# Half-by-half down projections, more plain tiles and in-place right factors in a hybrid decoder trunk

## The chip, the cores and the metric

The kernel runs on one core of a Trainium2 chip. The metric is the device time of one launch in microseconds. The core's engines are TensorE (PE; its weight loads are shown as PEld), VectorE (DVE), ScalarE (ACT), GpSimd (POOL) and SyncE (SP), which here issues all transfers.

## The reference

Two layers over 1024 prompt tokens and 8 sample tokens (1032 columns, model width 1024). Layer 0 mixes with windowed attention beside a recurrence (the even mixer), layer 1 with a gated chunk mixer (the odd mixer). Each mixer is followed by a ConvFFN of width 2816 (22 tiles of 128 rows). Every part is normed before and after:

```python
def conv_ffn(xn, conv_state, w_gate, w_up, conv_w, conv_b, w_down):
    gpre = xn @ w_gate
    ext = concatenate([conv_state, gpre], axis=1)
    conv = conv_b + conv_w[2] * ext[:, 2:2 + t]
    for j in range(2):
        conv = conv + conv_w[j] * ext[:, j:j + t]
    h = gelu(conv, approximate=True) * (xn @ w_up)
    return h @ w_down, ext[:, -2:]

for layer in range(2):
    m = even_mix(rmsnorm(h), ...) if layer % 2 == 0 else chunk_gmlp_mix(rmsnorm(h), ...)
    h = h + rmsnorm(m)
    h = h + rmsnorm(conv_ffn(rmsnorm(h), ...))
```

All data are float32. Besides the two outputs of the trunk, states and caches are returned.

## The kernel before

**Arithmetic.** Activations lie with features on the partitions and tokens along the columns. Every float32 operand is split into a high part, rounded to fp32r, and a low part (`split`, L283 to L286: ACT makes the high part, DVE or POOL subtracts it). A product is three matmuls, high by high, high by low, low by high (`mm3`, L288 to L291).

**Tokens.** The ConvFFN and the odd mixer treat the tokens in two halves: A is chunk 0 (512 columns), B is chunks 1 and 2 (256 and 264 columns). The operand of half A lies in the tiles `xA`, that of B in `xB`.

**ConvFFN.** `FFN_STEPS` lists the steps of each ConvFFN; `ffn` (L539) walks it.
- `up` steps (`gate_up`, *plain tiles*): gate and up projection of one 128-row tile f for one half. All A steps come first, then all B steps. The weights are split once, stored in DRAM (`wk<-w`), and reread for half B (`w<-wk`). The result h, split in two parts, goes to DRAM (`hd`).
- `pair` steps (`pair`, `both`): two tiles f, f+1 together over all tokens by seven block products instead of eight: the weight pair is a 2 by 2 block matrix (tile by half of the 1024 input rows), and so is the activation (half of the input rows by half of the 1032 tokens, blocks of 516 columns). The seven left factors are formed per pair from raw weights `wa` (`wfactor`, in VectorE's `ws` and in place). Three of the right factors are blocks of x themselves; the other four are sums of blocks and are made once per ConvFFN: `combos` makes three of them in `ta`, `yA`, `yB` and stores the fourth in DRAM (`t4d`), and `combo4` reads and splits it into `xB` buffers that the last plain B step has freed. `combos` is called after the first B step.
- `down` steps (`down`): `load_h` reads h back into `ta`, `gb`, `cb`; the products of the listed tiles add up in PSUM and are then added to y (`yA` for half A, `yB` for half B, L718). After the last one of a chunk, `Boundary.chunk` does the norm after the ConvFFN, the residual and, in the first one, the norm ahead of the odd mixer, whose operand it writes.

Before, the first ConvFFN has 6 plain tiles and 8 pairs, the second 4 and 9. Tiles 0 to 17 go down two at a time over all tokens, tiles 18 to 21 together, first for half A, then for half B.

**Buffers.** Tag `s` has four buffers, which `xc` (blocks of x in `combos`), `wa`, and the residual and norm tiles of the boundaries share. `ta`, `yA`, `yB` have four each, `gb`, `cb`, `ub` two each. Split weights rotate through 8 + 10 buffers of 128 by 512; the weights of a `down` tile take four. Weights are requested three loads ahead in plain and down steps, seven in pairs.

**Order.** The framework fixes the order of each engine's queue in advance, by priority in program order and by its own estimate of when things are ready. On the chip each engine runs its queue in that order and waits on semaphores. SP issues every transfer, so a transfer that must wait holds up those behind it.

Of the kernel before, what the change touches and what calls it, by code (L numbers as in the profile page):

```python
# [9 lines left out]
F32 = mybir.dt.float32  # L10
F32R = mybir.dt.float32r
# [5 lines left out]
P = 128  # L17
# [8 lines left out]
NF = 22  # L26
# [97 lines left out]
def trunk(ctx: ExitStack, tc: tile.TileContext, A, O):  # L124
# [375 lines left out]
    def ft(tag, n=TW, dt=F32):  # L500
        return pools[tag].tile([P, n], dt, tag=tag, name=nm(tag), bufs=FBUFS.get(tag, 1))
# [28 lines left out]
    def ffn(l, xs, raw, bnd):  # L530
# [29 lines left out]
        def gate_up(f, half):  # L560

            t0, n = FCH[half[0]][0], sum(FCH[c][1] for c in half)
            row = ft(("gb", "cb", "ub")[f % 3])
# [29 lines left out]
        def combos():  # L593

            xs.fill()
            for k in range(4):
                x = []
                for i, t0 in ((k, 0), (k, 2 * NQ), (4 + k, 0), (4 + k, 2 * NQ)):
                    t = stile("xc")[:, 0:2 * NQ]
                    SP.dma_start(out=t, in_=raw[i * P:(i + 1) * P, t0:t0 + 2 * NQ])  # L600
                    x.append(t)
                if k % 2 == 0:
                    for i, tag in enumerate(("ta", "yA", "yB")):
                        for part in range(2):
                            tt[i, part, k // 2] = ft(tag, TW, F32R)
                t3 = stile("t3", "g")[:, 0:2 * NQ]
                DVE.tensor_tensor(out=t3, in0=x[3], in1=x[1], op=ALU.subtract)
                DVE.tensor_tensor(out=x[1], in0=x[1], in1=x[0], op=ALU.subtract)
                DVE.tensor_tensor(out=x[3], in0=x[3], in1=x[1], op=ALU.subtract)
                DVE.tensor_tensor(out=x[2], in0=x[2], in1=x[3], op=ALU.subtract)  # L610
                SP.dma_start(out=t4d[k], in_=x[2])
                for i, src in enumerate((x[1], x[3], t3)):
                    split(src, *(tt[i, part, k // 2][:, k % 2 * 2 * NQ:(k % 2 + 1) * 2 * NQ] for part in range(2)),
                          POOL if i == 0 else DVE)
# [72 lines left out]
        def load_h(f):  # L687

            for s, half in enumerate(HALVES):
                t0, n = FCH[half[0]][0], sum(FCH[c][1] for c in half)  # L690
                for part in range(2):
                    t = ft("ta" if f % 4 == 0 else ("gb", "cb")[s], TW, F32R)
                    SP.dma_start(out=t[:, 0:2 * n].bitcast(F32).rearrange("p (i t) -> p i t", i=2),
                                 in_=hd[part][f:f + 2, :, t0:t0 + n].rearrange("i p t -> p i t"))
                    for c in half:
                        for i in range(2):
                            o = i * n + FCH[c][0] - t0
                            hs[f + i, c, part] = t[:, o:o + FCH[c][1]]

        def down(fs, cs, first, last):  # L700
            for f in range(fs[0], min(fs[-1] + 4, NF), 2):
                if (f, cs[0], 0) not in hs:
                    load_h(f)
# [19 lines left out]
        for kind, fs, cs in FFN_STEPS[l]:  # L723
            if kind == "up":
                gate_up(fs, cs)
                if cs == HALVES[1] and not ready:
                    combos()
                    ready = 1
            elif kind == "pair":
                if ready == 1:  # L730
                    combo4()
                    ready = 2
                pair(fs)
            else:
                down(fs, cs, 0 in fs, NF - 1 in fs)
# [38 lines left out]
def _ffn_steps(a, b):  # L774
# [7 lines left out]
    L = tuple(range(NF - b, NF))  # L782
    return s + [("down", L, A), ("down", L, B)]


FFN_STEPS = [_ffn_steps(*a) for a in ((6, 4), (4, 4))]
# [1025 lines left out]
```

## Time and profile before

| | |
|---|---|
| median of 3 runs | 2622.96 us (2621.48 to 2625.72) |
| the profiled execution's own time | 2619.32 us |
| its span, first to last instruction | 2617.5 us |
| mean granted TensorE clock | 0.961 |
| transfers | 509.33 MB, mean 195 GB/s |

How to read the views. Times are us from the span's start unless marked ns. A row of the timeline gives start, duration, engine, line, operation, out<-in with the program's tile names, partitions x elements, and in brackets the engine's idle time before it and what ended that. A row of the windows gives, for one stretch, the busy time of each engine with its number of instructions, then the granted share of TensorE's clock, the busy share of the 16 DMA engines and GB/s. Matmuls are pipelined: a matmul's duration overlaps the next one's, so the pace is read from starts. In the order of time the span has the even mixer (to about 840, overlapped by the first A steps from 719 on), the first ConvFFN (to 1508), the odd mixer (to 1910, overlapped by the second ConvFFN's A steps) and the second ConvFFN.

### The profile page before, as it was taken

The page shows a single profiled execution, that of the slowest core. Times are in us where ns is not written, and L with a number is a line of the kernel's source. Part 1 is how long each engine was busy: PE and PEld are TensorE (multiplying, and loading weights), DVE is VectorE, ACT ScalarE, POOL GpSimd, SP SyncE. Part 2 cuts the span into 40 slices and gives each one's busy share as a digit, 9 for nine tenths or more (in the row PEclk, how much of TensorE's full clock was granted, in tenths as well). Part 3 has the DMA queues.
Part 4 walks back from the last instruction along what each step waited for, and adds up shares of the span by engine and source line. Part 5 has one row for each costly group of instructions (what it writes and reads, how often), then busy time and mean ns, then how long its engine had stood idle before and what let it go on. Part 6 is the DMA issues. An engine that isn't in the chain of part 4 may idle for free. (4 is left out here: it accounts for less than half of the span.)

```text
span 2617.5 us, 50052 instructions
## 1 busy us (share of the span) xinstructions
PE 2446.7 (93%) x18604; PEld 2266.3 (87%) x18604; DVE 1643.1 (63%) x3571; ACT 986.9 (38%) x1941; POOL 873.5 (33%) x947
## 2 busy tenths in 40 slices
PE   6889998999887989999999979999978999999996
PEld 5788888888775989999999868998878999999996
DVE  5776859666764566676455566526566667654556
ACT  4453545444342344444311144434434444441111
POOL 1511123110333255555322253202425555542221
PEclk9899999999798999999999989999989999999998
DMA  9776767765599832323644688665963232354455
GB/s 317 266 241 209 218 193 233 223 213 161 192 345 330 271 107 100 120 92 125 232 133 152 225 283 278 206 190 193 331 214 120 89 120 90 110 190 154 146 186 186
DMA packets 310676, 509.33 MB, mean 195 GB/s; under 512 B 50784, under 2 KB 94368, under 8 KB 310432
## 3 DMA queue, kind: packets, MB, share of 16 engines
q1 hardware_dynamic: 310432, 506.14, 58.3%
q8 instruction: 146, 2.39, 0.4%
q14 instruction: 98, 0.80, 0.1%
HBM read 337.15 MB, written 166.22 MB: 192 GB/s over the span
## 5 line engine op out<-in xcount | busy, mean ns | idle before, releaser
L286 POOL TENSOR_TENSOR w<-raw,w 128x512 fp32r<-128x512 f32 x212 | 288.5, 1371 | 623.4 <-ACT w L285 573.0
L289 PE MATMUL l<-xA,w 128*128 128x258 f32 (+1 forms) x896 | 297.3, 333 | 19.8 <-ACT w L285 15.8
L285 ACT ACTIVATE w<-raw 128x512 fp32r<-128x512 f32 x232 | 143.1, 629 | 453.5 <-PE l L290 317.9
L291 PE MATMUL l<-xA,w 128*128 128x258 f32 (+1 forms) x896 | 295.9, 331 | 1.2 <-POOL w L286 1.0
L290 PE MATMUL l<-xA,w 128*128 128x258 f32 (+1 forms) x896 | 296.2, 331 | 0.6 <-DVE xA L286 0.6
L289 PE MATMUL le<-xs,w 128*128 128x256 f32 (+1 forms) x896 | 270.2, 302 | 24.9 <-ACT w L285 18.3
L289 PE MATMUL l<-xB,w 128*128 128x256 f32 (+2 forms) x976 | 277.4, 287 | 15.1 <-ACT xB L285 14.4
L290 PE MATMUL l<-xB,w 128*128 128x256 f32 (+2 forms) x976 | 279.4, 287 | 0.8 <-DVE xB L286 0.7
L291 PE MATMUL l<-xB,w 128*128 128x256 f32 (+2 forms) x976 | 278.9, 286 | 0.0
L291 PE MATMUL le<-xs,w 128*128 128x256 f32 (+1 forms) x896 | 268.6, 301 | 9.1 <-POOL w L286 6.0
L290 PE MATMUL le<-xs,w 128*128 128x256 f32 (+1 forms) x896 | 265.0, 296 | 0.6 <-DVE xs L286 0.6
L286 POOL TENSOR_TENSOR w<-wa,w 128x512 fp32r<-128x512 f32 x136 | 214.8, 1586 | 65.3 <-ACT w L285 65.3
L289 PEld LDWEIGHTS le<-xs,w 128*128 128x128 f32 x896 | 178.2, 199 | 38.0 <-ACT w L285 21.5
L289 PEld LDWEIGHTS l<-xA,w 128*128 128x128 f32 x896 | 171.6, 192 | 37.5 <-ACT w L285 18.3
L289 PEld LDWEIGHTS l<-xB,w 128*128 128x128 f32 x976 | 186.1, 192 | 16.4 <-ACT xB L285 15.4
L286 POOL TENSOR_TENSOR w<-ws,w 128x512 fp32r<-128x512 f32 x102 | 145.9, 1430 | 162.4 <-ACT w L285 144.4
L291 PEld LDWEIGHTS le<-xs,w 128*128 128x128 f32 x896 | 177.7, 199 | 17.4 <-POOL w L286 7.8
L290 PEld LDWEIGHTS l<-xB,w 128*128 128x128 f32 x976 | 187.0, 192 | 1.7 <-DVE xB L286 1.5
L291 PEld LDWEIGHTS l<-xB,w 128*128 128x128 f32 x976 | 187.2, 192 | 0.0
L291 PEld LDWEIGHTS l<-xA,w 128*128 128x128 f32 x896 | 171.0, 191 | 17.3 <-POOL w L286 1.8
L290 PEld LDWEIGHTS l<-xA,w 128*128 128x128 f32 x896 | 171.1, 191 | 16.0 <-DVE xA L286 1.3
L289 PE MATMUL l<-ta,w 128*128 128x512 f32 (+2 forms) x576 | 184.6, 320 | 0.1
(496 smaller groups left out, 6812.2 us busy)
## 6 DMA issues: line engine op xcount, KB each, us to landing
w<-wk SPq DMA_DIRECT2D x544, 256.0 KB, 4.0
wk<-w SPq DMA_DIRECT2D x320, 256.0 KB, 3.8
raw<-in_down_dram SPq DMA_DIRECT2D x88, 256.0 KB, 4.3
hd<-cb SPq DMA_DIRECT2D x34, 516.0 KB, 4.0
hd<-ub SPq DMA_DIRECT2D x34, 516.0 KB, 4.0
wa<-in_gate_dram SPq DMA_DIRECT2D x68, 256.0 KB, 2.8
wa<-in_up_dram SPq DMA_DIRECT2D x68, 256.0 KB, 2.6
ta<-hd SPq DMA_DIRECT2D x24, 520.0 KB, 5.4
```

Of the source, the lines that this page charges most:

```text
L285: ACT.activation(out=hi, in_=src, func=AF.Copy)
L286: (eng or DVE).tensor_tensor(out=lo, in0=src, in1=hi.bitcast(F32), op=ALU.subtract)
L289: PE.matmul(out, wh, xh, start=start, stop=False, **kw)
L290: PE.matmul(out, wh, xl, start=False, stop=False, **kw)
L291: return PE.matmul(out, wl, xh, start=False, stop=stop, **kw)
```

## The change

Three edits in the ConvFFN:

1. `FFN_STEPS`: plain tiles from 6 to 8 in the first ConvFFN and from 4 to 6 in the second (one pair fewer in each). The last eight tiles, not the last four, go down half by half: tiles 14 to 17 for A, 18 to 21 for A, 14 to 17 for B, 18 to 21 for B. `load_h` loads the halves that the present step and the next one need, through `ta`, `gb`, `ta`, `cb` in turn.
2. Plain tiles use the row buffers `gb` and `cb` in turn, no longer `ub`.
3. `combos` reads three of the four block rows two row blocks at a time into buffers of `ta`, `yA` and `yB` themselves (for both row pairs ahead), uses `ub` for two sums, and writes the split factors over buffers of the same tags. Only the fourth block passes through `xc`.

```diff
@@ gate_up
-            row = ft(("gb", "cb", "ub")[f % 3])
+            row = ft(("gb", "cb")[f % 2])
@@ combos
-            for k in range(4):
-                x = []
-                for i, t0 in ((k, 0), (k, 2 * NQ), (4 + k, 0), (4 + k, 2 * NQ)):
-                    t = stile("xc")[:, 0:2 * NQ]
-                    SP.dma_start(out=t, in_=raw[i * P:(i + 1) * P, t0:t0 + 2 * NQ])
-                    x.append(t)
-                if k % 2 == 0:
-                    for i, tag in enumerate(("ta", "yA", "yB")):
-                        for part in range(2):
-                            tt[i, part, k // 2] = ft(tag, TW, F32R)
-                t3 = stile("t3", "g")[:, 0:2 * NQ]
-                DVE.tensor_tensor(out=t3, in0=x[3], in1=x[1], op=ALU.subtract)
-                DVE.tensor_tensor(out=x[1], in0=x[1], in1=x[0], op=ALU.subtract)
-                DVE.tensor_tensor(out=x[3], in0=x[3], in1=x[1], op=ALU.subtract)
-                DVE.tensor_tensor(out=x[2], in0=x[2], in1=x[3], op=ALU.subtract)
-                SP.dma_start(out=t4d[k], in_=x[2])
-                for i, src in enumerate((x[1], x[3], t3)):
-                    split(src, *(tt[i, part, k // 2][:, k % 2 * 2 * NQ:(k % 2 + 1) * 2 * NQ] for part in range(2)),
-                          POOL if i == 0 else DVE)
+            tags, W = ("ta", "yA", "yB"), 2 * NQ
+            def load(t, k, right, cnt):
+                SP.dma_start(out=cols(t, cnt, W), in_=rows(raw, k, cnt, right * W, W))
+                return t[:, 0:cnt * W]
+            x = {k: [load(ft(tag), r, right, 2) for tag, r, right in zip(tags, (k, k, 4 + k), (0, 1, 1))] for k in (0, 2)}
+            for k in (0, 2):
+                for i, tag in enumerate(tags):
+                    for part in range(2):
+                        tt[i, part, k // 2] = ft(tag, TW, F32R)
+                x11, x12, x22 = x[k]
+                t1, t2 = (ft("ub")[:, 0:2 * W] for _ in range(2))
+                DVE.tensor_tensor(out=t1, in0=x12, in1=x11, op=ALU.subtract)
+                DVE.tensor_tensor(out=t2, in0=x22, in1=t1, op=ALU.subtract)
+                for i in range(2):
+                    one = slice(i * W, i * W + W)
+                    t3 = stile("t3", "g")[:, 0:W]
+                    DVE.tensor_tensor(out=t3, in0=x22[:, one], in1=x12[:, one], op=ALU.subtract)
+                    x21 = load(stile("xc"), 4 + k + i, 0, 1)
+                    DVE.tensor_tensor(out=x21, in0=x21, in1=t2[:, one], op=ALU.subtract)
+                    SP.dma_start(out=t4d[k + i], in_=x21)
+                    split(t3, *(tt[2, part, k // 2][:, one] for part in range(2)), POOL)
+                for i, t in enumerate((t1, t2)):
+                    split(t, *(tt[i, part, k // 2][:, 0:2 * W] for part in range(2)))
@@ load_h, down, the walk over the steps
-        def load_h(f):
-            for s, half in enumerate(HALVES):
-                t0, n = FCH[half[0]][0], sum(FCH[c][1] for c in half)
-                for part in range(2):
-                    t = ft("ta" if f % 4 == 0 else ("gb", "cb")[s], TW, F32R)
...
+        halfs = [0]
+        def load_h(fs, cs):
+            for half in HALVES:
+                t0, n = FCH[half[0]][0], sum(FCH[c][1] for c in half)
+                for f in fs[::2] if half[0] in cs and (fs[0], half[0], 0) not in hs else ():
+                    for part in range(2):
+                        t = ft(("ta", "gb", "ta", "cb")[halfs[0] % 4], TW, F32R)
...
+                    halfs[0] += 1
-            for f in range(fs[0], min(fs[-1] + 4, NF), 2):
-                if (f, cs[0], 0) not in hs:
-                    load_h(f)
+                for _, f, c in FFN_STEPS[l][k:k + 2]:
+                    load_h(f, c)
@@ _ffn_steps
-    L = tuple(range(NF - b, NF))
-    return s + [("down", L, A), ("down", L, B)]
-FFN_STEPS = [_ffn_steps(*a) for a in ((6, 4), (4, 4))]
+    return s + [("down", tuple(range(f, f + 4)), half) for half in (A, B) for f in range(NF - b, NF, 4)]
+FFN_STEPS = [_ffn_steps(*a) for a in ((8, 8), (6, 8))]
```

## Rows read from the trace of the kernel before

**Rows 1.** The page: busy time, share and instructions of each engine.
```profile
PE 2446.7 (93%) x18604; PEld 2266.3 (87%) x18604; DVE 1643.1 (63%) x3571; ACT 986.9 (38%) x1941; POOL 873.5 (33%) x947
```
**Rows 2.** Windows, plain B steps and pairs: PE, PEld, DVE, ACT, POOL, clock, DMA share, GB/s.
```profile
860.00:910.00 50.00, 50.00 (x419) 50.00 (x418) 29.68 (x50) 17.60 (x38) 8.37 (x9) 1.00 0.89 286
...
1000.00:1200.00 200.00, 200.00 (x1667) 199.95 (x1667) 139.15 (x197) 84.69 (x137) 108.54 (x89) 1.00 0.31 106
```
**Rows 3.** Timeline of TensorE, ten consecutive matmuls of an A step, first and last.
```profile
1867.82 0.40 PE L291 MATMUL l<-xA,w 128*128 128x512 f32 x1
...
1869.90 0.39 PE L291 MATMUL l<-xA,w 128*128 128x512 f32 x1
```
**Rows 4.** Windows at the ConvFFNs' beginnings and ends, columns as in rows 2.
```profile
840.00:850.00 10.00, 0.00 (x0) 0.00 (x0) 0.74 (x2) 0.63 (x1) 0.18 (x1) 0.69 1.06 382
850.00:860.00 10.00, 8.95 (x49) 8.65 (x50) 5.60 (x8) 5.72 (x10) 3.33 (x8) 0.62 0.82 249
...
910.00:950.00 40.00, 33.32 (x257) 32.49 (x257) 23.92 (x36) 17.30 (x37) 20.87 (x18) 0.96 0.41 134
...
1500.00:1530.00 30.00, 15.40 (x86) 13.22 (x85) 24.63 (x40) 12.58 (x22) 18.27 (x13) 0.72 0.82 279
1890.00:1920.00 30.00, 18.12 (x111) 16.70 (x111) 19.41 (x53) 7.83 (x14) 6.15 (x5) 0.72 0.73 243
1950.00:2040.00 90.00, 75.15 (x568) 73.72 (x567) 53.91 (x77) 35.06 (x61) 44.07 (x39) 0.91 0.37 120
```
**Rows 5.** Timeline of TensorE, the longest waits in these windows.
```profile
850.91 0.58 PE L289 MATMUL l<-xB,w 128*128 128x256 f32 x1 [12.33 <-ACT xB L285]
...
942.69 0.44 PE L289 MATMUL l<-yB,w 128*128 128x258 f32 x1 [4.08 <-DVE gb L654]
...
1513.89 1.84 PE L331 MATMUL pp<-cst,sq 128*128 128x1 f32 x8 [5.60 <-DVE sq L325]
1522.68 1.08 PE L352 MATMUL pp<-cst,pp 128*128 128x128 f32 x4 [6.96 <-DVE pp L310]
1525.34 2.07 PE L289 MATMUL l<-xA,w 128*128 128x512 f32 x4 [1.57 <-ACT xA L285]
...
1904.33 1.11 PE L331 MATMUL pp<-cst,sq 128*128 128x1 f32 x6 [7.79 <-DVE sq L329]
...
1962.23 0.58 PE L289 MATMUL l<-xA,w 128*128 128x258 f32 x1 [5.88 <-ACT w L285]
```
**Rows 6.** Timeline of SP's queue, end of `combos` in the second ConvFFN.
```profile
1953.64 0.32 SPq L600 DMA_DIRECT2D xc<-xne  x1
1958.45 2.95 SPq L214 DMA_DIRECT2D wa<-in_gate_dram  x2
```
**Rows 7.** Timeline of VectorE, three places.
```profile
1482.96 0.69 DVE L718 TENSOR_TENSOR yA<-yA,l 128x512 f32<-128x512 f32 x1 [0.64 <-PE l L291]
...
1969.96 0.69 DVE L220 TENSOR_TENSOR ws<-wa,wa 128x512 f32<-128x512 f32 x1 [5.73 <-DMA wa<-in_gate_dram]
...
2598.37 0.43 DVE L329 TENSOR_TENSOR sq<-sq 128x264 f32<-128x264 f32 x1
```
**Rows 8.** The page's DMA issues: number, KB each, us from issue to landing.
```profile
w<-wk SPq DMA_DIRECT2D x544, 256.0 KB, 4.0
wk<-w SPq DMA_DIRECT2D x320, 256.0 KB, 3.8
...
ta<-hd SPq DMA_DIRECT2D x24, 520.0 KB, 5.4
```
**Rows 9.** Windows: last four tiles' down projections, half A into half B.
```profile
1480.00:1500.00 20.00, 19.87 (x157) 19.27 (x155) 12.04 (x30) 3.51 (x6) 5.49 (x5) 1.00 0.46 151
```
**Rows 10.** Timeline of TensorE, the end: sums of the last two norms.
```profile
2593.68 0.50 PE L331 MATMUL pp<-cst,sq 128*128 128x1 f32 x4
...
2604.07 1.11 PE L331 MATMUL pp<-cst,sq 128*128 128x1 f32 x6 [3.41 <-DVE yB L472]
```
**Rows 11.** Windows: ten us of the first A steps, beside the even mixer's end.
```profile
730.00:740.00 10.00, 9.72 (x60) 8.54 (x60) 8.01 (x23) 5.06 (x12) 2.54 (x2) 1.00 1.06 393
```

More of the change, by code (lines that the diff above doesn't have):

```diff
@@ L685, in pair @@
                 keep(f + i, u, c, u, 0)
-        def load_h(f):
-            for s, half in enumerate(HALVES):
+        halfs = [0]
+        def load_h(fs, cs):
+            for half in HALVES:
                 t0, n = FCH[half[0]][0], sum(FCH[c][1] for c in half)
-                for part in range(2):
-                    t = ft("ta" if f % 4 == 0 else ("gb", "cb")[s], TW, F32R)
[L693 to L698, printed above, removed]
+                for f in fs[::2] if half[0] in cs and (fs[0], half[0], 0) not in hs else ():
+                    for part in range(2):
+                        t = ft(("ta", "gb", "ta", "cb")[halfs[0] % 4], TW, F32R)
+                        SP.dma_start(out=t[:, 0:2 * n].bitcast(F32).rearrange("p (i t) -> p i t", i=2),
+                                     in_=hd[part][f:f + 2, :, t0:t0 + n].rearrange("i p t -> p i t"))
+                        for c in half:
+                            for i in range(2):
+                                o = i * n + FCH[c][0] - t0
+                                hs[f + i, c, part] = t[:, o:o + FCH[c][1]]
+                    halfs[0] += 1
         def down(fs, cs, first, last):
-            for f in range(fs[0], min(fs[-1] + 4, NF), 2):
-                if (f, cs[0], 0) not in hs:
-                    load_h(f)
             ws = [wget(f"down{l}", f) for f in fs]
@@ L722, in ffn @@
         ready = 0
-        for kind, fs, cs in FFN_STEPS[l]:
+        for k, (kind, fs, cs) in enumerate(FFN_STEPS[l]):
             if kind == "up":
```

## The prediction

> **What bounds the kernel now.** The page comes first: TensorE is busy 93% of the span, no other engine over 63% [rows 1]. A mean over unlike stages says little, so next come windows over the stages. Inside the ConvFFNs TensorE has no idle time at all: 419 matmuls in 50 us of plain B steps, 1667 in 200 us of pairs, so 0.120 us for one of 256 to 264 columns [rows 2]; one of 512 columns starts every 0.231 us (nine starts in 2.08 us) [rows 3]. There the count of matmuls is the time, and only doing fewer or narrower ones helps. All that is lost around these stages is lost at five joints [rows 4], and the timeline of TensorE says what each waits for [rows 5]. The loss of a joint is its window minus matmuls times pace.
>
> - **J1**, first ConvFFN, A steps to B steps (838 to 860): 12.33 us without a matmul, waiting for the operand `xB` of half B; then 49 matmuls (5.9 us at full pace) in the 9.1 us left of the window, at a granted clock of 0.62: 3.2 us. 15.5 us.
> - **J2**, its first pair: 40 - 257 x 0.120 = 9.2 us, the largest wait for VectorE's adds of `gb`.
> - **J3**, first ConvFFN to odd mixer: 74 wide matmuls of its 86, 63 x 0.120 + 11 x 0.231, and 0.4 for the small ones, 10.5 us in 30: 19.5 us, mostly the norm of half A (5.60 and 6.96 us before its sums and its spread), partly clock (0.72).
> - **J4**, second ConvFFN, A to B: 96 wide ones of its 111, 84 x 0.120 + 12 x 0.231, and 0.6 for the small, 13.5 us in 30: 16.5 us; 7.79 us of it before the norm's sums of the last chunk.
> - **J5**, its first pairs: 90 - 568 x 0.120 = 21.8 us; the largest wait (5.88) is for a weight's split.
>
> Together 82.5 us. The end is a sixth place: the norm of half B after the last matmul.
>
> **Two more plain tiles per ConvFFN.** One pair is replaced by two plain tiles. A pair issues 2 x 7 x 4 x 3 x 2 = 336 matmuls: 40.3 us. A plain tile issues 48 of 512 columns (11.1 us, an A step) and 96 of 256 or 264 (11.5 us, a B step), so two take 45.2 us. Price: 4.8 us per ConvFFN, **+9.6 us**, certain wherever TensorE is the bound. The Trainium skill (TensorE: Matmul & The Clock Gate, section Back-to-back issue gap) speaks for a lower price: it gives a sustained 131 ns for N=512. By that an A step would be 6.3 us and the swap would give back 4.7 us per ConvFFN instead of costing 4.8; the trace has 231 ns in these fp32r streams, so the measurement decides and the sum keeps +9.6.
>
> What it buys is independent work. J1 and J4 open because the A steps run out (6 and 4 of them) before half B's operand is there. Two more give 22.2 us of matmuls that need half A alone, against joints of 15.5 and 16.5 us, slow clock included. Bounds: nothing regained (15.5 and 16.5 stay) to everything. The added A tile is not free for the queues: 1.05 MB of raw weights, 2.1 MB of split weights kept in DRAM and 0.5 MB of result, 3.7 MB in 11.1 us or 330 GB/s, while J1's windows already move 382 and 249 GB/s. I leave 4 us at J1 and 3 at J4: **-11.5 and -13.5**.
>
> The two more B steps come after `combos` was called, so the right factors and the first pair's weights get 23 us more before they are needed. This counts for J2 and J5, below.
>
> **Row buffers.** Plain tiles now use `gb` and `cb` alone: four rows instead of six. A row lives from its first eviction, through one step, to the landing of its store, some 20 us; four last four steps, over 44 us. Cost 0, hidden by the steps between; if stores took 20 us longer it would be a wait per step.
>
> **Right factors in place.** Before, the 16 `xc` loads go through the four buffers of tag `s`, which the raw weights `wa` of the pairs need too. SP shows it: the last `xc` is issued at 1953.64, the first `wa` at 1958.45 [rows 6], and VectorE waits until 1969.96 for a gate weight [rows 7]. After, twelve of the sixteen blocks go straight into `ta`, `yA`, `yB`, and only four pass through `s`. The arithmetic stays (the same subtractions and splits, many twice as wide, so fewer instructions); the loads are six of double size and four single ones. So `wa` can be loaded during the B steps. SP runs past six larger loads early in the B steps; the weights behind them are three loads ahead, so a delay of a few us is covered. In-place use adds one wait: the low parts of the second row pair's third factor must wait until the block beneath was read, about 3 us on POOL, behind which only further splits queue; with five further B steps, 58 us, or more until the first pair it is covered. What stays late is the fourth factor, which needs the last plain step's buffers, and its four splits on VectorE. I leave 3 us at J2 and 4 at J5: **-6.2 and -17.8**. Bounds: 0 to -31 together.
>
> **Last eight down projections by halves.** The `hd` loads now run one step ahead instead of two; a step lasts 22 us and a load lands in 5.4 [rows 8], so 0. The same number of matmuls comes in four-tile steps A1, A2, B1, B2 instead of two-tile steps and one A, one B step. Half A is now complete 46 us (384 x 0.120) before half B, formerly 23 us. Its norm took from its last add at 1482.96 [rows 7] to the first matmul of the next stage at 1525.34, 42.4 us, so it nearly fits beneath B1 and B2 and J3 almost closes. Against it: four more tiles' weights are split, stored and read again, 4.2 MB each way, beside the norm's 4 MB of loads and stores; J3's window moves 279 GB/s as it is. Bounds 0 and -19.5; I take **-14.5**. Partial sums are added 24 times fewer per ConvFFN; VectorE was not the bound there, so 0.
>
> A step of four tiles holds 16 of the 18 weight buffers, so the next one's weights come late. The one such joint that a ConvFFN has before shows no loss in the first: 19.87 of 20 us busy [rows 9]. But its second half was a reread, while A1 to A2 also needs ACT's and POOL's splits, and B1 frees its buffers only in its second chunk. Four new joints, 0 to 12.7 us each (4.2 MB at 330 GB/s); nearer the row at 0: **+5** in all.
>
> In the last ConvFFN the same step moves half A's norm away from the end. There the last chunk's squares are summed at 2598.8 [rows 7], but TensorE's sums start at 2604.07, because the bank is still read for the chunk before [rows 10], and that one was late behind half A's work. **-5**, bounds 0 and -8.
>
> **Sum.** 9.6 + 5 - 11.5 - 6.2 - 14.5 - 13.5 - 17.8 - 5 = -53.9. The profiled execution took 2619.3 us (span 2617.5 and 1.8 around it): 2565.4. The median of the runs is 3.6 higher: 2569. All bounds at their best (-82.5 - 8 + 9.6) give 2542.
>
> **The rivals.**
> - *R1, DMA is the limit at the joints.* The change adds 64 kept stores and 64 rereads to 320 and 544 [rows 8], 33.6 MB at 262 KB each. Then the added transfers push back what J1, J3 and J4 wait for, and these three stay: -53.9 + 11.5 + 14.5 + 13.5 = -14.4, 2609. For it: J1's wait lies in a window at full DMA share. Against it: the A steps before J4 keep their pace [rows 3]. The Trainium skill (DMA: Bandwidth & Descriptors, section Bandwidth) puts HBM's limit per core near 358 GB/s; by that 33.6 MB would be 94 us of transfers, had they no cover. The trace has 393 GB/s over 10 us [rows 11], above that figure.
> - *R2, TensorE's fixed order.* Its queue is written in advance; if the norm's sums stand ahead of the new A steps, TensorE still waits at J1 and J4 with work behind: -53.9 + 25 = -28.9, 2594. For it: J4's wait is exactly at such sums, `pp<-cst,sq`. Against it: the queue had no other work to put there.
> - *R3, the first pairs are late for other reasons* (VectorE's in-order queue): J2 and J5 stay, -53.9 + 24 = -29.9, 2593. For it: J2's largest wait is VectorE's. Against it: J5's largest is a weight.
> - *R4, slower.* No weight of a four-tile step arrives before the step ahead of it ends: 12.7 us at six joints, 76 us instead of 5: -53.9 + 71 = +17, 2640. It decides from 9.8 us a joint on (58.9 / 6). Against it: the existing joint at no loss.
>
> **How the numbers follow.** Forecast 0.57 (its own range 2545 to 2588), R1 0.12, R2 0.12, R3 0.10, R4 0.06, no net change 0.03. 0.2% (5 us) is about what a measurement of this kernel tells from no change. Faster is all but R4, the no-change case and a part of R1: 0.89; same 0.03; slower 0.08. The range runs from the best bounds to past R2 and R3, leaving out R4 and most of R1: 2542 to 2604.
>
> **What would show it.** Right: no TensorE wait over 3 us between A and B steps in either ConvFFN; `wa` issued during the B steps; TensorE busy between the last down projection and the odd mixer; 18508 matmuls with more busy time in the ConvFFNs; 384 kept stores, 608 rereads; the end within 20 us of the last wide matmul. Wrong: waits on `w<-wk` or on splits at A1 to A2 or B1 to B2 (R4); waits for `xB` with DMA at full share (R1); waits at `pp<-cst,sq` with A steps behind (R2).

## The result, and the profile after

The changed kernel takes 2595.15 us (median of 4 runs, 2588.62 to 2601.36); the kernel before, run beside it, 2624.34 us (2621.48 to 2625.99). The ratio is 0.989, 95% interval 0.9863 to 0.9916: some 29 us faster, where 54 were forecast. The time lies in the range given (2542 to 2604), near its slow end, and outside the range that the forecast gave for itself (2545 to 2588). The profiled execution took 2596.03 us, its span 2594.2 us against 2617.5.

The page of the changed kernel, TensorE's line and three lines of the DMA issues (number, KB each, us from issue to landing):

```profile
PE 2450.8 (94%) x18508; PEld 2263.8 (87%) x18508; DVE 1600.0 (62%) x3471; ACT 982.8 (38%) x1937; POOL 863.2 (33%) x943
...
w<-wk SPq DMA_DIRECT2D x608, 256.0 KB, 4.1
wk<-w SPq DMA_DIRECT2D x384, 256.0 KB, 3.7
...
ta<-hd SPq DMA_DIRECT2D x36, 512.0 KB, 4.6
```

96 matmuls fewer than in [rows 1], 64 kept stores and 64 rereads more than in [rows 8]: the change does what it says. Windows of the changed kernel, columns as in [rows 2]:

```profile
860.00:910.00 50.00, 34.01 (x237) 32.37 (x238) 31.73 (x40) 18.91 (x34) 14.38 (x17) 0.86 1.01 360
870.00:880.00 10.00, 4.81 (x24) 4.56 (x24) 8.87 (x7) 3.42 (x5) 4.05 (x2) 0.60 1.06 393
960.00:1010.00 50.00, 50.00 (x417) 49.93 (x416) 32.70 (x50) 23.39 (x44) 26.40 (x24) 1.00 0.27 87
1440.00:1460.00 20.00, 16.19 (x63) 12.51 (x62) 4.67 (x9) 4.41 (x8) 4.80 (x4) 0.91 1.03 389
1460.00:1510.00 50.00, 43.77 (x310) 41.52 (x309) 37.94 (x79) 13.73 (x22) 13.07 (x9) 0.93 0.76 265
1510.00:1560.00 50.00, 49.69 (x288) 43.37 (x287) 38.53 (x75) 22.42 (x37) 27.53 (x22) 1.00 0.83 281
1900.00:1930.00 30.00, 28.54 (x178) 25.33 (x177) 20.76 (x44) 10.23 (x19) 6.36 (x10) 1.00 1.02 363
1960.00:2050.00 90.00, 88.97 (x739) 88.77 (x739) 56.17 (x85) 38.90 (x71) 44.19 (x41) 1.00 0.40 136
2510.00:2560.00 50.00, 44.78 (x312) 42.43 (x311) 22.70 (x53) 3.36 (x6) 5.16 (x5) 0.90 0.74 252
```

Against [rows 4], four joints are closed or nearly so: the first pairs of both ConvFFNs (960 to 1010, 1960 to 2050), the way to the odd mixer (1510 to 1560), and A to B in the second ConvFFN (1900 to 1930). One is as open as before: 860 to 910 holds 237 matmuls where [rows 2] has 419 in 50 us, and the granted clock is 0.60 in 870 to 880, which holds the last 4 us of the stall. And there are losses where there were next to none: 1440 to 1510 and 2510 to 2560, at the four-tile down steps. TensorE's timeline there, the longest waits:

```profile
874.27 0.55 PE L289 MATMUL l<-xB,w 128*128 128x256 f32 x1 [10.16 <-DMA w<-wk]
881.40 0.80 PE L289 MATMUL l<-xB,w 128*128 128x264 f32 x2 [2.33 <-ACT xB L285]
...
1451.43 0.79 PE L289 MATMUL l<-gb,w 128*128 128x512 f32 x1 [3.72 <-ACT w L285]
1477.56 0.74 PE L291 MATMUL l<-cb,w 128*128 128x256 f32 x4 [3.57 <-DMA w<-wk]
1479.78 0.58 PE L289 MATMUL l<-ta,w 128*128 128x256 f32 x1 [1.48 <-DVE yB L725]
...
1920.36 0.51 PE L289 MATMUL l<-xB,w 128*128 128x264 f32 x2 [1.46 <-ACT xB L285]
...
2574.11 0.28 PE L291 MATMUL l<-gb,w 128*128 128x264 f32 x1
...
2580.62 1.11 PE L331 MATMUL pp<-cst,sq 128*128 128x1 f32 x6 [6.23 <-DVE sq L329]
```

The first line is the point. J1 of [rows 5] waited 12.33 us for the operand `xB`; that wait is gone, and in its place TensorE waits 10.16 us for weights that are reread. The last two lines are the tail: the last wide matmul starts at 2574.11, the span ends 20.1 us later, where 23.8 us lay before (from the sums at 2593.68 in [rows 10], which stand right behind the last wide matmul, to the end of the span).

**One account for all kernels.** Loss of a window = its length minus 0.120 us for each matmul of 256 to 264 columns and 0.231 for each of 512, counted by start; the small matmuls of the norms count as loss. Each row comes from one execution. An example: 840 to 940 of the changed kernel has 84 of 512 and 474 of 256 to 264 columns, 100 - 19.4 - 56.9 = 23.7 us. "End" is the last 100 us of the span. The names are those of the experiments below.

| kernel | 840-940 (J1) | 940-1010 (J2) | 1430-1560 (down steps, J3) | 1880-1940 (J4) | 1940-2060 (J5) | end | sum |
|---|---|---|---|---|---|---|---|
| before | 19.4 | 4.5 | 24.0 | 18.0 | 22.2 | 26.4 | 114.5 |
| changed | 23.7 | 0.2 | 21.1 | 4.6 | 2.0 | 32.2 | 83.8 |
| plain tiles alone | 9.2 | 6.3 | 25.0 | 4.4 | 12.1 | 25.9 | 82.9 |
| combos alone | 26.3 | 0.2 | 23.2 | 20.0 | 1.3 | 26.7 | 97.7 |
| half by half alone | 18.9 | 6.9 | 26.6 | 18.5 | 22.0 | 33.8 | 126.7 |
| changed, old combos | 8.1 | 4.5 | 22.7 | 3.6 | 10.6 | 33.6 | 83.1 |
| changed, old down steps | 23.8 | 0.2 | 24.6 | 4.7 | 1.9 | 25.8 | 81.0 |
| changed, later call | 22.6 | 0.2 | 20.9 | 5.9 | 2.3 | 32.0 | 83.9 |
| later call, old down steps | 22.0 | 0.2 | 25.1 | 5.8 | 1.7 | 24.7 | 79.5 |
| later call, two-tile steps | 24.7 | 0.2 | 19.7 | 4.4 | 1.7 | 29.9 | 80.6 |
| loads held back | 11.4 | 0.0 | 22.0 | 3.8 | 2.0 | 34.3 | 73.5 |
| held back, old down steps | 11.9 | 0.2 | 25.0 | 4.0 | 2.3 | 25.5 | 68.9 |
| held back, mixed steps | 12.0 | 0.2 | 12.3 | 3.7 | 2.2 | 27.4 | 57.8 |
| the same, first ConvFFN alone | 9.3 | 0.0 | 13.0 | 3.6 | 2.2 | 26.3 | 54.4 |

For the change as a whole: 114.5 - 83.8 = 30.7 us less, minus the 9.6 us of added matmul time, is 21.1; the span is 23.3 shorter. Ahead of these windows two executions differ with nothing changed there: the same A steps end at 857.2 us in the kernel with the later call and at 865.8 in the one with mixed steps. So the table says where time went, and the timed ratios say how much.

### The profile page after: what moved, and what is told of

Its sections match the earlier page's. It is cut to its first block, busy times and chain, and to the rows that moved or that the text cites. A ratio compares the mean times of both kernels' runs of the same rounds, so it can differ in the third digit from the quotient of the medians.

```text
span 2594.2 us, 49897 instructions
## 1 busy us (share of the span) xinstructions
PE 2450.8 (94%) x18508; PEld 2263.8 (87%) x18508; DVE 1600.0 (62%) x3471; ACT 982.8 (38%) x1937; POOL 863.2 (33%) x943
## 4 chain that ended last, share of the span: by engine, by line
PE 77%; DVE 9%; DMA 6%; issue 3%; POOL 2%; ACT 2%; SPq 1%; DVEq 0%; POOLq 0%; ACTq 0%
PE l L289 17%; PE l L290 17%; PE l L291 17%; PE le L291 3%; PE le L289 3%; PE le L290 3%; PE m L291 2%; PE m L289 2%; PE m L290 2%; DMA w<-wk 2%; POOL w L286 1%; PE ch L1490 1%; PE ch L1493 1%; DMA raw<-in_win_even_dram 1%; PE pr L1380 1%
## 5 line engine op out<-in xcount | busy, mean ns | idle before, releaser
L286 POOL TENSOR_TENSOR w<-raw,w 128x512 fp32r<-128x512 f32 x228 | 310.8, 1373 | 603.1 <-ACT w L285 546.6
L289 PE MATMUL l<-xB,w 128*128 128x256 f32 (+2 forms) x1072 | 303.2, 286 | 18.7 <-DMA w<-wk 10.2
L285 ACT ACTIVATE w<-raw 128x512 fp32r<-128x512 f32 x248 | 153.4, 628 | 417.6 <-PE l L290 257.0
L289 PE MATMUL l<-xA,w 128*128 128x258 f32 (+1 forms) x896 | 301.8, 337 | 6.5 <-ACT w L285 5.9
L291 PE MATMUL l<-xA,w 128*128 128x258 f32 (+1 forms) x896 | 301.9, 337 | 3.5 <-POOL w L286 3.3
L291 PE MATMUL l<-xB,w 128*128 128x264 f32 (+2 forms) x1072 | 305.2, 286 | 0.0
L290 PE MATMUL l<-xB,w 128*128 128x264 f32 (+2 forms) x1072 | 304.8, 285 | 0.0
L290 PE MATMUL l<-xA,w 128*128 128x258 f32 (+1 forms) x896 | 301.6, 337 | 0.6 <-DVE xA L286 0.6
L289 PEld LDWEIGHTS l<-xB,w 128*128 128x128 f32 x1072 | 203.0, 191 | 20.5 <-ACT yA L285 10.6
L286 POOL TENSOR_TENSOR w<-wa,w 128x512 fp32r<-128x512 f32 x120 | 187.8, 1571 | 74.2 <-ACT w L285 65.4
L289 PEld LDWEIGHTS le<-xs,w 128*128 128x128 f32 x896 | 178.1, 199 | 37.9 <-ACT w L285 22.4
L290 PEld LDWEIGHTS l<-xB,w 128*128 128x128 f32 x1072 | 204.4, 191 | 0.2
L291 PEld LDWEIGHTS l<-xB,w 128*128 128x128 f32 x1072 | 204.1, 190 | 0.1
L291 PEld LDWEIGHTS le<-xs,w 128*128 128x128 f32 x896 | 177.6, 199 | 17.7 <-POOL w L286 8.1
L289 PEld LDWEIGHTS l<-xA,w 128*128 128x128 f32 x896 | 169.6, 189 | 25.6 <-ACT w L285 7.4
L291 PEld LDWEIGHTS l<-xA,w 128*128 128x128 f32 x896 | 169.5, 189 | 22.5 <-POOL w L286 4.6
L290 PEld LDWEIGHTS l<-xA,w 128*128 128x128 f32 x896 | 169.4, 189 | 18.0 <-DVE xA L286 0.7
L290 PEld LDWEIGHTS le<-xs,w 128*128 128x128 f32 x896 | 178.3, 199 | 4.6 <-issue 2.1
L725 DVE TENSOR_TENSOR yA<-yA,l 128x512 f32<-128x512 f32 x128 | 87.5, 687 | 149.7 <-PE l L291 149.7
```

Of the source, the lines that this page charges most:

```text
L285: ACT.activation(out=hi, in_=src, func=AF.Copy)
L286: (eng or DVE).tensor_tensor(out=lo, in0=src, in1=hi.bitcast(F32), op=ALU.subtract)
L289: PE.matmul(out, wh, xh, start=start, stop=False, **kw)
L290: PE.matmul(out, wh, xl, start=False, stop=False, **kw)
L291: return PE.matmul(out, wl, xh, start=False, stop=stop, **kw)
L725: DVE.tensor_tensor(out=yc, in0=yc, in1=ps[:, :n], op=ALU.add)
```

## The experiments

**Theories ahead of the first runs.** Theory 1: what is left at J1 comes from the six large x loads of the new `combos`, which stand on SP's queue among the first B steps' rereads. Theory 2: the rereads and the added A tiles fill the transfers there by themselves. Theory 3: the half-by-half steps give back at their joints what they save at J3 and at the end. SP's timeline of the changed kernel is where Theory 1 is from:

```profile
849.54 0.71 SPq L599 DMA_DIRECT2D ta<-xnd  x1
...
851.61 0.76 SPq L599 DMA_DIRECT2D ta<-xnd  x1
...
863.62 0.37 SPq L599 DMA_DIRECT2D yA<-xnd  x1
...
864.94 0.37 SPq L599 DMA_DIRECT2D yB<-xnd  x1
865.57 0.37 SPq L599 DMA_DIRECT2D yA<-xnd  x1
...
876.77 0.37 SPq L599 DMA_DIRECT2D yB<-xnd  x1
```

516 KB each, 3.2 MB, issued from 849 on, while the weights of the first B steps, rereads issued from 857 on, are still on their way and the transfers run at 393 GB/s (the window 870 to 880 above).

**The parts alone, and all but one.** First the changed kernel with the old `combos`, shown against the changed kernel (plain tiles keep their two row buffers here, unlike what the expectation says):

```diff
-            x = {k: [load(ft(tag), r, right, 2) for tag, r, right in zip(tags, (k, k, 4 + k), (0, 1, 1))] for k in (0, 2)}
...
+                    t = stile("xc")[:, 0:2 * NQ]
+                    SP.dma_start(out=t, in_=raw[i * P:(i + 1) * P, t0:t0 + 2 * NQ])
```

> The changed kernel with the old building of the combinations (third part of the change undone; the three shared row buffers come back with it). Theory 1: the stall that stayed at the first B steps of the first ConvFFN comes from the six large x loads that the new combos puts on SP's queue ahead of the first B steps' repeated weights. Then here the wait there falls from 10.2 us to under 3 us and the loss of 860 to 910 us from some 18 us to 8 or less, while the losses at the first pairs (J2 and J5, some 30 us together) come back: about 2612 us. Theory 2: the two added A tiles and the repeated weights alone use up the transfers there; then the stall stays at 10 us or more, and the time is about 2623 us, as before the change.

2596.11 us, ratio 0.9914 (0.9891 to 0.9937). The wait at the first B step is 5.41 us for `w<-wk`, not 10.2 and not under 3; the loss of 840 to 940 is 8.1 us instead of 23.7. J2 and J5 come back, but only by 12.9 us of some 30, since the added plain tiles help at J5 too (12.1 instead of 22.2 by themselves); that is why it is 16 us faster than Theory 1 had it. On top of the plain tiles the new `combos` gains these 12.9 us and loses 15.6 at J1.

The kernel before with the new `combos` and two row buffers, all else as before; against the changed kernel:

```diff
-FFN_STEPS = [_ffn_steps(*a) for a in ((8, 8), (6, 8))]
+FFN_STEPS = [_ffn_steps(*a) for a in ((6, 4), (4, 4))]
```

(with the old `load_h` and `_ffn_steps`.)

> The kernel before with the new building of the combinations and two row buffers, the old steps (6 and 4 plain tiles, four tiles in the last down steps). Both theories: J2 and J5 close, some 28 us less. Theory 1: the x loads in front of the repeated weights lengthen the stall at the first B steps from 15.5 us to over 20 us: about 2603 us. Theory 2: that stall doesn't change: about 2596 us.

2606.49 us, ratio 0.9946 (0.9924 to 0.9968). J2 and J5 close; J1 still waits 12.61 us for `xB`, and its window loses 26.3 us against 19.4, though J2's part is gone from it. The time lies nearer Theory 1's number (2603 and 2596 were expected), though the nine runs spread from 2594 to 2614. Its mechanism is not what this kernel shows: no wait for `w<-wk` stands between 850 and 910. After the first wait four more follow, 7.3 us in all, every one for `xB`; two of them:

```profile
860.08 0.58 PE L289 MATMUL l<-xB,w 128*128 128x256 f32 x1 [2.26 <-ACT xB L285]
...
867.76 0.58 PE L290 MATMUL l<-xB,w 128*128 128x256 f32 x1 [2.99 <-DVE xB L286]
```

The splits that make `xB` run on ScalarE and VectorE among the sums of `combos`; VectorE is busy 10.00 of the 10 us from 860 to 870, and the granted clock is 0.51 from 845 to 873. So as far as these rows show, the new `combos` costs here through its arithmetic, a second way that none of the theories names.

The kernel before with the half-by-half steps alone; against the kernel before:

```diff
-FFN_STEPS = [_ffn_steps(*a) for a in ((6, 4), (4, 4))]
+FFN_STEPS = [_ffn_steps(*a) for a in ((6, 8), (4, 8))]
```

(`load_h` and the down steps of the change; old `combos`, three row buffers.)

> The kernel before with the last eight down projections half by half (steps of four tiles, their kept rows read half by half), old combinations, 6 and 4 plain tiles. As the prediction has it: J3 closes (14.5 us less), the four new joints cost 5 us, the end gives 5 us: about 2610 us. Theory 3: the four-tile steps' joints cost what the changed kernel shows there, some 30 us in all, against some 20 us of J3 and 4 us at the end that they give: about 2630 us, no gain at all.

2638.43 us, ratio 1.007 (1.0043 to 1.0098): slower, and by more than Theory 3 said. 1430 to 1560 loses 2.6 us more, the end 7.4 more. These 10 of the 19 us are placed. Another 5.7 lie ahead of the first B steps: the A steps end at 843.9 us instead of 838.2, although TensorE and SP run the same instructions in the same order up to there. So the edit doesn't explain the length of that stretch in the profiled execution, and not all of the 19 us is shown to be the price of the steps.

The kernel before with two more plain tiles per ConvFFN and nothing else; against the kernel before:

```diff
-FFN_STEPS = [_ffn_steps(*a) for a in ((6, 4), (4, 4))]
+FFN_STEPS = [_ffn_steps(*a) for a in ((8, 4), (6, 4))]
```

> The kernel before with two more plain tiles in each ConvFFN alone (8 and 6). It costs 9.6 us of matmul time for certain. Theory 1: without the early x loads J1 closes (11.5 us less) and so does J4 (13.5 us less): about 2609 us. Theory 2: J1 stays, J4 closes: about 2620 us.

2593.1 us, ratio 0.9899 (0.9878 to 0.9921): as fast as the whole change, and better than expected. J1 falls to 9.2 (a wait of 4.68 us for `w<-wk`), J4 to 4.4, and J5 by 10, since the later first pair helps it too. The two other parts together add nothing measurable to this one.

The changed kernel without its half-by-half steps; from here on diffs are against the changed kernel:

```diff
-FFN_STEPS = [_ffn_steps(*a) for a in ((8, 8), (6, 8))]
+FFN_STEPS = [_ffn_steps(*a) for a in ((8, 4), (6, 4))]
```

(with the old `load_h` and `_ffn_steps`.)

> The changed kernel without its half-by-half down projections (first part undone): 8 and 6 plain tiles, the new combinations, four tiles and all tokens in the last down step. Theory 3: the half-by-half steps give back at their joints (some 30 us in both ConvFFNs) what they save at J3 and at the end (some 20 to 25 us): 2588 us, a little faster than the changed kernel. As the prediction had it (J3 14.5 and the end 5 saved, joints 5): about 2610 us. The stall at the first B steps stays near 10 us in both.

2590.2 us, ratio 0.9898 (0.9878 to 0.9919). Theory 3's number, 20 us from the prediction's: 1430 to 1560 loses 3.5 us more than the changed kernel, the end 6.4 less.

**When the six loads are issued.** The call of `combos` moved from the first B step to the fourth, in the source:

```diff
-                if cs == HALVES[1] and not ready:
+                if cs == HALVES[1] and fs == 3 and not ready:
                     combos()
```

> The changed kernel with the new building of the combinations called after the fourth B step instead of after the first: the same six large x loads, four smaller loads and the same sums, about 35 us later. Theory 1: the stall before the first B step (10.2 us behind repeated weights) falls to 5 us or less and the loss of 860 to 910 us to 9 or less, and the first pairs still find their factors ready: about 2585 us. Theory 2 (the repeated weights alone fill the transfers there): no change there, 2595 us. A third outcome, the factors late at the first pairs for the later start: J2 comes back, 2595 us or more, with waits at the first products.

2597.98 us, ratio 0.9931 (0.991 to 0.9952): no gain, and 11.05 us of wait for `w<-wk`. By its expectation this spoke for Theory 2. SP's timeline of this run says that nothing was tested, first and last of the six:

```profile
842.60 0.75 SPq L599 DMA_DIRECT2D ta<-xnd  x1
...
870.82 0.37 SPq L599 DMA_DIRECT2D yB<-xnd  x1
```

The stall ends at 868.29 here, so five of the six loads still go out ahead of the first B step. The framework places each instruction by when it believes it can run; a load whose buffer is free is ready long before the call. The same move with the old down steps:

```diff
-                if cs == HALVES[1] and not ready:
+                if cs == HALVES[1] and fs == 3 and not ready:
                     combos()
...
-FFN_STEPS = [_ffn_steps(*a) for a in ((8, 8), (6, 8))]
+FFN_STEPS = [_ffn_steps(*a) for a in ((8, 4), (6, 4))]
```

> Both of the others together: no half-by-half steps, and the combinations built after the fourth B step. Theories 1 and 3: some 10 us less than without the later call, 2578 us, the fastest so far. Theory 2: as without the later call, 2588 us.

2591.56 us, ratio 0.9913 (0.9889 to 0.9936), J1 at 22.0: as without the move.

So the loads were given something to wait for: one element of the third B step's row is copied into the target of each load of the first ConvFFN.

```diff
             def load(t, k, right, cnt):
+                if gate is not None:
+                    POOL.tensor_copy(out=t[:, 0:1], in_=gate[:, 2:3])
                 SP.dma_start(out=cols(t, cnt, W), in_=rows(raw, k, cnt, right * W, W))
...
-                gate_up(fs, cs)
-                if cs == HALVES[1] and not ready:
-                    combos()
+                row = gate_up(fs, cs)
+                if cs == HALVES[1] and fs == (2, 0)[l] and not ready:
+                    combos((row, None)[l])
```

> The changed kernel with the ten x loads of the first ConvFFN's combinations held back: one element of the third B step's row is copied into each load's tile first, so that no load can start before that step is done (the second ConvFFN as in the changed kernel). Theory 1: the six large loads between the repeated weights cause the rest of the stall at the first B steps; with them gone from there the wait behind repeated weights falls from 10.2 us to about 5 us, as in the two kernels with the old building, the low clock after it goes, and the loss of 860 to 910 us falls from 18 us to 9 or less: about 2585 us. Theory 2: the repeated weights fill the transfers alone: wait 10 us, 2595 us. If the factors come late at the first pairs instead, waits of 5 us and more stand at the first products there, and the time is 2595 us or more.

2580.18 us, ratio 0.9861 (0.9834 to 0.9888). SP's timeline, the first and the last of the six loads; TensorE's, the start of the B steps; and two windows of this kernel:

```profile
904.23 0.37 SPq L602 DMA_DIRECT2D ta<-xnd  x1
...
908.51 0.90 SPq L602 DMA_DIRECT2D yB<-xnd  x1
```

```profile
865.18 0.55 PE L289 MATMUL l<-xB,w 128*128 128x256 f32 x1 [4.44 <-DMA w<-wk]
```

```profile
860.00:910.00 50.00, 45.56 (x359) 45.07 (x358) 16.97 (x33) 15.30 (x33) 5.55 (x25) 0.93 0.92 324
870.00:880.00 10.00, 10.00 (x86) 10.00 (x85) 2.13 (x3) 2.69 (x5) 0.18 (x1) 1.00 1.06 387
```

Same rereads, same kept stores, same DMA share of 1.06 between 870 and 880, but 86 matmuls there instead of 24 (the stall also begins 3.4 us earlier here). The wait is 4.44 us instead of 10.16, the loss of 840 to 940 is 11.4 instead of 23.7, and J2 stays closed. Theory 1 holds for the wait for rereads: it is 10.2 to 11.4 us in the five kernels that have both the early loads and the added plain tiles, and 4.4 to 5.4 in the six that have the plain tiles without the early loads. Theory 2 is left with these 4.4 to 5.4 us.

Holding the loads back also holds back the sums and splits of `combos` that need them. In the changed kernel two further waits stand behind these: 2.33 us for `xB` (the second line of TensorE's waits in the section on the result; ScalarE's split comes after one that waited for VectorE's sum) and 2.67 us at 906.06 for VectorE's `gb`. They go as well. Of the 12 us, 5.7 are the shorter wait for rereads; no run separates the loads from the sums for the rest.

With the old down steps as well:

```diff
-FFN_STEPS = [_ffn_steps(*a) for a in ((8, 8), (6, 8))]
+FFN_STEPS = [_ffn_steps(*a) for a in ((8, 4), (6, 4))]
```

(the holding back as above, the old `load_h` and `_ffn_steps`.)

> The same with the half-by-half down projections undone (eight and six plain tiles, new combinations, loads held back, last four down tiles in one step for all tokens). Theories 1 and 3: about 10 us less than without the holding back, 2580 us, J3 (some 20 us) still there.

2576.63 us, ratio 0.984 (0.9814 to 0.9866), as expected.

**What the four-tile steps wait for.** The changed kernel with the later call and two tiles in each half step:

```diff
-    return s + [("down", tuple(range(f, f + 4)), half) for half in (A, B) for f in range(NF - b, NF, 4)]
+    return s + [("down", (f, f + 1), half) for half in (A, B) for f in range(NF - b, NF, 2)]
...
-                for _, f, c in FFN_STEPS[l][k:k + 2]:
+                for _, f, c in FFN_STEPS[l][k:k + (2 if cs == HALVES[0] + HALVES[1] else 4)]:
```

> The changed kernel with the later combinations and with its last eight down tiles half by half in steps of two tiles instead of four: eight weight buffers a step instead of sixteen, the same loads, kept copies and repeated reads, twice the additions into the rows. Theory 3a: the joints stall because a four-tile step holds 16 of the 18 weight buffers until its second half; with two tiles the next step's weights are there, the losses of 1440 to 1510 us (18 us) and 2510 to 2560 us (12 us) fall under 5 each: some 20 to 25 us less than with four tiles, 2562 us. Theory 3b: the kept copies' 4.2 MB out and 4.2 MB in per ConvFFN take the transfers whatever the step is: no gain from smaller steps, 2585 us.

2592.34 us, ratio 0.9913 (0.9892 to 0.9934): some 6 us better than the four-tile kernel with the same call, by medians whose intervals overlap, and not the 20 to 25 expected. TensorE's waits from 1440 to 1520 (us in total, times, longest), in the changed kernel:

```profile
PE l L291 <- DMA w<-wk: 4.5, 2, 3.6
PE l L289 <- ACT w L285: 3.7, 1, 3.7
PE l L289 <- DVE yB L725: 1.5, 1, 1.5
PE l L289 <- DMA w<-wk: 0.3, 1, 0.3
```

and with two tiles a step:

```profile
PE l L289 <- DVE yB L725: 9.6, 7, 2.9
```

Theory 3a is right about the buffers: with the same bytes, every wait behind a weight or its split is gone in this stretch. But another wait took its place. VectorE's timeline of this run:

```profile
1471.59 5.36 DVE L472 SCALAR_TENSOR_TENSOR yA<-yA,vec,pp 128x512 f32<-128x512 f32 x8
1476.86 1.42 DVE L725 TENSOR_TENSOR yB<-yB,l 128x264 f32<-128x264 f32 x4
```

Eight operations of half A's norm stand in one run ahead of four additions into half B's row. In 5.36 us TensorE makes seven more products of a two-tile step (6 matmuls of 0.120 us each), and then waits until an addition has read its bank; of a four-tile step it would make under four.

That gave the last form: two tiles a step for half A, where no norm runs yet, then one step of four and two of two for half B, with the loads held back.

```diff
+    s += [("down", (f, f + 1), A) for f in range(NF - b, NF, 2)]
+    L = NF - b
+    return s + [("down", tuple(range(L, L + 4)), B)] + [("down", (f, f + 1), B) for f in range(L + 4, NF, 2)]
...
+                ahead = 0
+                for _, f, c in FFN_STEPS[l][k:]:
+                    ahead += len(f) // 2 * (2 if len(c) == 3 else 1)
+                    if ahead > 4:
+                        break
+                    load_h(f, c)
```

> Loads held back, and the last eight down tiles half by half with steps of different size: two tiles a step for the first half of the tokens, then one step of four tiles and two of two for the second half. Theory 3a, as the run with two tiles everywhere left it: weight buffers stall a four-tile step after a four-tile step, and steps of two tiles next to the boundary's norm stall on the row additions behind it on VectorE (9.6 us in 1440 to 1560 us). Four tiles just there halve the additions: no wait behind weights over 1.5 us, additions under 4 us in all, the losses of 1440 to 1520 and 2510 to 2560 us 8 us or less each: about 2570 us, the fastest. If the norm delays the additions of four tiles just as much, nothing is gained on the run with two tiles: 2582 us.

2570.83 us, ratio 0.9815 (0.9787 to 0.9843). Its only waits of TensorE from 1440 to 1520:

```profile
PE l L289 <- DVE yB L728: 3.1, 4, 1.0
```

1430 to 1560 loses 12.3 us instead of 24.0: the 12 us that the prediction had wanted from the change itself, with no wait there longer than 1.0 us. The waits are as expected, the loss is not: 1440 to 1520 loses 10.4 us, where 8 or less were expected. The end loses 27.4, still no less than before. Against the same kernel without half-by-half steps (2576.63) this is 6 us by medians, with intervals that overlap.

Last, the half-by-half steps in the first ConvFFN alone, all else as in the run before:

```diff
+    if b == 4:
+        L = tuple(range(NF - b, NF))
+        return s + [("down", L, A), ("down", L, B)]
...
-FFN_STEPS = [_ffn_steps(*a) for a in ((8, 8), (6, 8))]
+FFN_STEPS = [_ffn_steps(*a) for a in ((8, 8), (6, 4))]
```

> The fastest so far (loads held back, two tiles a step for the first half of the tokens, then four, two and two), with the half-by-half steps in the first ConvFFN alone; the second one ends as before the change (four tiles, first half, then second half). Theory: half by half pays only where another boundary's matmuls wait for the first half of the tokens, so at J3 and not at the end, where the loss from 2500 us on was 17.1 us with it and 15.9 us in the run without it; also 4.2 MB fewer copies go out and come back: 2570 us, within 4 us of the fastest. Rival, the prediction's term for the end: half by half saves 5 us there, so that this one takes 2575 us or more, with a tail longer by 5 us behind the last wide matmul.

2562.3 us, ratio 0.9794 (0.9772 to 0.9816), the fastest median of all and 33 us under the changed kernel's (27 when each is set against the kernel before that ran beside it); its interval overlaps the one of the run before, so this step alone is not measured as faster, only as no slower. The rival's 2575 us or more did not come. TensorE's timeline at the end of this kernel:

```profile
2536.04 0.50 PE L331 MATMUL pp<-cst,sq 128*128 128x1 f32 x4
2542.18 0.66 PE L352 MATMUL pp<-cst,pp 128*128 128x128 f32 x2 [5.63 <-DVE pp L310]
2546.25 1.11 PE L331 MATMUL pp<-cst,sq 128*128 128x1 f32 x6 [3.41 <-DVE yB L472]
```

The tail is 23.8 us (2536.0 to 2559.8), as before the change. So half by half as the change has it does shorten the tail, by 3.7 us between these two profiles, and what it costs ahead of the tail is more. Counted from the start of the last wide matmul, the tail is 19.6 to 20.2 us in the five kernels with four-tile half-by-half steps in the second ConvFFN and 21.6 to 24.3 in the seven without such steps there: 3 us on average.

## Why the prediction came out as it did

The bound was read rightly: TensorE's count of matmuls plus five joints, with 18508 matmuls as foretold. The terms against the table (forecast, measured):

- **Plain tiles, +9.6, and J4, -13.5.** Right: J4 18.0 to 4.6, -13.4. (45.2 - 40.3 is 4.9 for each ConvFFN and 9.8 in all; nothing hangs on the 0.2.) The added A steps run at their pace and cover what half B waits for; plain tiles alone show the same. R2 (TensorE's fixed order) is refuted: it would have kept J4.
- **J5, -17.8.** Right: 22.2 to 2.0, -20.2, with `wa` issued during the B steps as foretold (from 1957.04 on; the first pair's first matmul starts at 1987.4). R3 (first pairs late for other reasons) is refuted.
- **J1 and J2 together, -17.7.** Wrong: the two windows lose 23.9 us before and 23.9 after (the wait of the kernel before begins 1.4 us ahead of its window). J2 did close, and the wait for `xB` at J1 did go. The step that failed is "SP runs past six larger loads early in the B steps; the weights behind them are three loads ahead, so a delay of a few us is covered". The loads go out ahead of the B steps, not in them, between rereads that are needed at once, and the transfers were already full. Held back, with the sums that need them, they leave 11.4 us in these windows, so this one step cost some 12 us, of which 5.7 are the wait for rereads itself. A short wait for rereads remains at 4.4 us; that it is the transfers' limit is argued from the DMA share of 0.92, not shown.
- **J3, -14.5, with two of the four new joints, +2.5.** Mis-sized: 24.0 to 21.1, -2.9 instead of -12. The gap before the odd mixer closed (49.69 of 50 us busy), so the mechanism was right; the joints took it back: 1440 to 1510 loses 18.4 us where +2.5 stood. "Nearer the row at 0" was the wrong choice between the bounds. [rows 9] was not quite at 0 either: by the account above its 20 us lose 1.6, which a busy share of 19.87 doesn't show. And it has a four-tile step followed by the same tiles and half B, with half A's norm still to come. The new joints have fresh splits (3.72 us), rereads behind kept stores (3.57 us) and the norm's work beside the row additions (1.48 us), and the clock falls behind them (0.91 and 0.93 in the two windows).
- **The end, -5, with the two other joints, +2.5.** Mis-sized, and on the other side of nothing: 26.4 to 32.2. The tail did get 3.7 us shorter; 2510 to 2560, with the joints, loses 11.2 us.
- **R1 (DMA is the limit at the joints)** had J1, J3 and J4 stay. J1 stayed as its condition said, in windows at full DMA share, but for the loads of `combos` ahead of the rereads and not for the 33.6 MB added: with these bytes still moved and the loads held back, 12 of the 24 us go. J3 and J4 closed.
- **R4 (slower)** needed 9.8 us a joint. The six joints of the changed kernel come to 29.6 us, some 5 each: 5.9 in 1440 to 1460, 12.5 for two in 1460 to 1510, 11.2 for the second ConvFFN in 2510 to 2560. The sum had +5 for the four new ones. R4's mechanism is there at under half of its 12.7 us a joint; with it the half-by-half steps alone were slower than before, the whole was not.

Summed: -53.9 forecast, 17.7 + 9.1 + 8.3 us off at J1 and J2, J3, and the end, 2.3 us to the good at J4 and J5: -21.1 by the table, -23.3 in the span.

That the time fell into the range is in part luck. 2595 is some 2 us or less from R2's 2594 and R3's 2593, and the rows refute both; the range reaches this time because it was drawn to cover them. Of the sum, the plain tiles, J4 and J5 came out as worked out, J1 and J2 together gave nothing, and the joints cost six times what they were given. The signs said so too: of those for "right", the one that no wait between A and B steps is over 3 us failed (10.16), and one of those for "wrong" came, a wait on a split at A1 to A2 (3.72).

## What to carry to other kernels

A load that is moved earlier or made larger is costed against what is queued and needed right behind it, at the place where the scheduler really puts it; moving the call in the source may move nothing, a data dependence does. A bigger step that holds nearly all buffers of its kind can stall at a change of step, and a smaller one can stall on the adds that it doubles: size each step by which of the two engines has other work at that moment. Time every part of a change alone: here one line gave as much as the whole; the new `combos` paid only after what it had made late was found and moved (2576.63 us against 2593.1), and what the half-by-half steps add to that is 6 to 14 us by medians, with intervals that still touch.

## What the runs showed of the hardware beyond that

- A stall costs more than its length, and in the two cases here the short one cost nearly as much on top as the long one. Waits of 17.1 us in 860 to 910 (10.16, 2.33, 2.67, 1.33 and 0.63) make a loss of 20.2 by the account above, 3.1 more; in the kernel with the loads held back 4.44 us make 6.9, 2.5 more. The granted clock fell in both: with the stall that ends at 874.27 it is 0.50 in 870 to 875 and 0.71 in 875 to 880, with the one that ends at 865.18 it is 0.79 in 860 to 865 and 0.53 in 865 to 870 (0.50 is 1.2 GHz, 1.00 is 2.4).
- Transfers were faster than the 393 GB/s of [rows 11] over whole stretches: of the 40 slices that the DMA view of the changed kernel cuts 1440 to 1510 into (1.75 us each), fifteen move 399 GB/s or more, the highest 410. The Trainium skill (HBM Reference, section Specifications (TRN2)) has a core that streams alone at about 425 GB/s, bounded by its DMA engines, and about 358 as the share when both cores of a pair stream; the trace agrees with the first.

```profile
GB/s 311 405 406 405 405 399 317 406 407 405 405 407 409 138 15 307 273 273 345 406 402 392 403 393 350 224 160 149 151 0 0 180 321 361 351 308 243 191 410 178
```
